# Queue orders by hand behind the head of a hybrid mLSTM and sparse-attention block

## The chip, the cores and the metric

One core of a Trainium2 chip runs the whole program. The metric is the device time of one execution in microseconds: 527.67 us for the kernel before (median of three runs, 526.49 to 528.49).

## The reference

A decoder block for 512 tokens of width 1024, all in fp32, cut to what matters:

```python
u = rmsnorm(x, norm_in)
m_q, m_k, m_v, m_o, m_z, m_if, a_q, a_k, a_v, a_z, ix_q, ix_k, ix_w = split(u @ w_in)   # 1024 x 6736
mq, mk = split(silu(causal_dwconv(concat(m_q, m_k), conv_w)))          # 4 taps
hm = mlstm_chunkwise(mq, mk, m_v, log_i, log_sigmoid(f))               # 4 heads, 128 x 256
hm = sigmoid(m_o) * rmsnorm_per_head(hm) * m_norm * silu(m_z)
score = sum_h ix_w[h] * relu(ix_q[h] . ix_k)                           # 8 indexer heads
idx = top_k(causal(score), 128)                                        # per query
ha = softmax(a_q.a_k / 8 + rel_bias, over idx) @ a_v                   # 8 heads of 64
h = x + concat(hm, ha * silu(a_z)) @ w_out                             # 1536 x 1024
h = h + (p @ w_ple) * sigmoid(h @ w_ple_gate)                          # 256 / 1024 x 1024
out = rmsnorm(h) * norm_final
```

## The kernel before

**Products.** Every operand of a product is split into a rounded high part and a low part (the difference), and a product is three matmuls of 128x128 by up to 512 columns: high by high, high by low, low by high. `dense_fm` (L200) makes four banks of one product side by side with the weights stationary, `dense_tm` (L222) does the same with the activations stationary. Weights come in slabs of 128x1024 elements through the SP queue (`load`); `split` (L143) makes a slab's high part on ScalarE (L148) and its low part on VectorE, or on GpSimd for the 14 even slabs from 8 to 34 (L149, `POOLP`). `feed` keeps loads four slabs and splits one slab ahead of the product; four slabs of a product take a bank from empty to full.

**Stages.** The head (to about 40 us) transposes x, normalises, splits u and makes the indexer's queries (`iq`) and the small product `mps` (indexer keys, gates). Then come the products mq, mk (conv inputs), mv in two halves, o and z in two halves, av, the attention's q and k by pairs of heads (`aqk`), az, the output projection `wo` in two halves, and the gate `wg` in two halves. Around them run: the indexer's scores (24 units of two matmuls, a relu, a multiply-add), its top-k (16 rounds of MAX8 and MATCH_REPLACE8 for three blocks of queries, L524 and L525), the convolutions (eight times three multiply-adds, a tanh, a multiply-add; L450 to L453), the gate sequences (scans), the mLSTM (per head four state-score steps and four numerator steps) and the attention (32 units of head and query block).

**What sets the order.** The head stands in `tc.manual_schedule`, so the compute engines run it in source order. Behind it, Tile's scheduler orders each engine's instructions by priority and by its own estimate of when they are ready; `urgent()` raises the priority of what empties a PSUM bank. In the source, side work is a list `back` of generators; each product calls `beat()` every six matmuls, which adds one credit and runs the first generator for as many steps as the credit pays (`COST_SC` 1.3 per score, `COST_CV` 1.5, `COST_TK` 1.5 per top-k pair). `weave` runs the mLSTM or the attention as the main line with two, or 1.4, six-matmul pieces of a product after each step. PSUM has four banks `mm` for the products and four banks `x` for all else. At run time each engine takes its queue strictly in the order that was fixed.

**What to follow.** `evac_iq` (L271) empties each iq bank in two halves: ScalarE copies 64 partitions (L278), VectorE subtracts (L279), then the same for the other half. L411 to L415 do so for the indexer's keys and then make the gate rows with ScalarE (`rows`, from the same bank `mps`). `evac_mv` (L537) empties a bank of mv with ScalarE (L545) and VectorE (L546). `evac_gate1` (L900) is the last stage's end: per block of 128 tokens it gates two halves of 256 columns, takes a power on GpSimd (L909), scales and stores. `values` of the attention multiplies a head's transposed weights with its values `LAG2` units after the last transpose (`flip`).

Of the kernel before, what the change touches and what calls it, by code (L numbers as in the profile page):

```python
# [47 lines left out]
def block_kernel(ctx: ExitStack, tc: tile.TileContext, x, p, w_in, b_gate, conv_w, w_out, norm_in,  # L48
# [121 lines left out]
    back, credit = [], [0.0]  # L170

    def beat():

        credit[0] += 1.0
        while back and credit[0] >= 0.0:
            cost = next(back[0], None)
            if cost is None:
                back.pop(0)
            else:
                credit[0] -= cost  # L180
        if not back:
            credit[0] = 0.0
# [17 lines left out]
    def dense_fm(nb, evac, tok0=0, name="fm"):  # L200
# [4 lines left out]
        while k0 < KT:  # L205
            h, l = piece()
            nk = h.shape[1]
            for b in range(nb):
                bs = slice(b * P, (b + 1) * P)
                for k in range(nk):  # L210
# [6 lines left out]
                    if k % 2:  # L217
                        beat()
                        yield
            k0 += nk  # L220

    def dense_tm(aH, aL, kts, evac, name="tm"):  # L222

        banks = [mm_bank(f"{name}{i}") for i in range(NT)]
        for k0 in range(0, len(kts), KP):
            sub = kts[k0:k0 + KP]
            h, l = piece()
            for i in range(NT):
# [6 lines left out]
                if k0 + KP >= len(kts):  # L235
                    evac(i, banks[i])
                beat()
                yield
# [88 lines left out]
    with tc.manual_schedule(engines={EN.PE, EN.DVE, EN.Activation, EN.Pool}):  # L327
# [33 lines left out]
        for kt in range(KT):  # L361
# [57 lines left out]
    iw_ps = x_bank("iw_ps")  # L419
    for i in range(1, NT):  # L420
        T.transpose(iw_ps[:, i * 12:(i + 1) * 12], rw[0][64:76, i * P:(i + 1) * P], ident[64:76, 64:76])
    V.tensor_copy(iwt[:, 1:, :], iw_ps[:, 12:48].rearrange("p (i c) -> p i c", c=12))

# [5 lines left out]
    tv_ps = x_bank("tv_ps")  # L429
    T.matmul(tv_ps[0:AH, :], rb, oh, start=True, stop=True)  # L430
    tv = sp.tile([P, SW], F32, tag="sH", bufs=1, name="tv")[0:AH, 0:S]
    V.tensor_copy(tv[:, 0:256], tv_ps[0:AH, 0:256])
    V.memset(tv[:, 256:S], BIG)

    tdram = dp.tile([AH, P, S], F32, name="tdram")
    nc.scalar.dma_start(tdram[:, :, 0:384], tv[:, 0:384].rearrange("h (o c) -> h o c", o=1).to_broadcast([AH, P, 384]))
# [10 lines left out]
    def conv(c, raw):  # L447
        y = mqk[c]
        for j in range(1, 4):
            V.scalar_tensor_tensor(y[:, j:], raw[:, 0:S - j], cw(3 - j, c), y[:, j:], op0=OP.mult, op1=OP.add)  # L450
        yield COST_CV
        A.activation(raw, y, AF.Tanh, scale=0.5)
        V.scalar_tensor_tensor(y, raw, 1.0, y, op0=OP.add, op1=OP.mult)  # L453
        yield COST_CV

    def evac_qk(c0):
        def go(b, ps):
# [3 lines left out]
            with urgent():  # L461
                A.activation(raw, ps, AF.Copy)
                A.activation(y, ps, AF.Copy, scale=cw(3, c))
# [12 lines left out]
    def sequences():  # L476
        A.activation(fr[1], fr[0], AF.Abs)
        A.activation(fr[2], fr[1], AF.Exp, scale=-1.0)
        A.activation(fr[1], fr[2], AF.Ln, bias=1.0)
        yield 1.0  # L480
        V.scalar_tensor_tensor(lr[2], fr[0], 0.0, fr[1], op0=OP.min, op1=OP.subtract)
        V.tensor_tensor_scan(lr[1], lr[2], lr[0], 0.0, op0=OP.add, op1=OP.max)
        yield 1.0
# [3 lines left out]
        for j in range(NT):  # L487
            n = S - j * P
            seg = ar[:, OFF[j]:OFF[j] + n]
            V.tensor_tensor_scan(seg, ones[64:76, :].to_broadcast([12, n]), lr[2][:, j * P:], 0.0, op0=OP.mult, op1=OP.add)  # L490
            V.tensor_tensor(lr[3][:, j * P:(j + 1) * P], lr[0][:, j * P:(j + 1) * P], seg[:, 0:P], OP.subtract)
            V.tensor_tensor(seg, seg, lr[1][:, j * P:], OP.subtract)
            yield 1.0
        nc.scalar.dma_start(adram, arow[72:76, 0:1280])
# [4 lines left out]
    def scores():  # L499
        for i in range(1, NT):  # L500
            n = (i + 1) * P
            sc = keep(f"sc{i}", shape=(P, n))
            for h in range(IH):
# [5 lines left out]
                A.activation(r, ps, AF.Relu)  # L509
                w = iwt[:, i, h:h + 1]  # L510
                if h == 0:
                    V.tensor_scalar(sc, r, w, None, op0=OP.mult)
                else:
                    V.scalar_tensor_tensor(sc, r, w, sc, op0=OP.mult, op1=OP.add)  # L514
                yield COST_SC
            G.affine_select(out=sc[:, i * P:], in_=sc[:, i * P:], compare_op=OP.is_ge, fill=-1e38, base=0,  # L516
                            pattern=[[-1, P]], channel_multiplier=1)
            sel[i] = sc

    def topk():  # L520
# [6 lines left out]
        for i in range(1, NT):  # L527
            V.tensor_scalar(sel[i], sel[i], -2e38, BIG, op0=OP.is_gt, op1=OP.mult)
        ended[0] = True

    back += [scores(), sequences(), topk()]
# [5 lines left out]
    def evac_mv(c):  # L537
        def go(i, ps):
# [3 lines left out]
            with urgent():  # L542
                G.memset(f(vH[i, c])[:, :, MV:], 1.0)
                G.memset(f(vL[i, c])[:, :, MV:], 0.0)
                A.activation(vH[i, c][:, :, 0:MV], src, AF.Copy)  # L545
                V.tensor_tensor(vL[i, c][:, :, 0:MV], src, f(vH[i, c])[:, :, 0:MV], OP.subtract)  # L546
# [6 lines left out]
    gc_ps = x_bank("gc_ps")  # L553
    for q, r in ((0, 3), (1, 1)):
        for i in range(NT):
            o = (q * NT + i) * 12
            T.transpose(gc_ps[:, o:o + 12], lr[r][:, i * P:(i + 1) * P], ident[64:76, 64:76])
    gc = gc_ps[:, 0:96].rearrange("p (q i c) -> p q i c", q=2, c=12)
    V.tensor_copy(gcol[:, 0], gc[:, 0, :, 8:12])

    V.tensor_scalar(gcol[:, 1], gc[:, 1, :, 8:12], -43.0, None, op0=OP.max)
    A.activation(gcol[:, 1], gcol[:, 1], AF.Exp, scale=-2.0)
    V.tensor_scalar(gcol[:, 1], gcol[:, 1], EPS, None, op0=OP.mult)
# [4 lines left out]
    def evac_o(b0):  # L568
        def ev(b, ps):
            go[b0 + b] = keep(f"go{b0 + b}")  # L570
            with urgent():
                A.activation(go[b0 + b], ps, AF.Tanh, scale=0.5)
        return ev

    def evac_z(b0):
        def ev(b, ps):
            sz = tmp("sz")
            g = go[b0 + b]
            with urgent():
                A.activation(sz, ps, AF.Tanh, scale=0.5)  # L580
                V.scalar_tensor_tensor(sz, sz, 1.0, ps, op0=OP.add, op1=OP.mult)
            V.scalar_tensor_tensor(g, g, 1.0, sz, op0=OP.add, op1=OP.mult)
# [9 lines left out]
    def split_mix(h):  # L592
        for c in (2 * h, 2 * h + 1):
            mixH[c], mixL[c] = keep(f"mixH{c}", F32R), keep(f"mixL{c}", F32R)
            A.activation(mixH[c], go[c], AF.Copy)
            V.tensor_tensor(mixL[c], go[c], f(mixH[c]), OP.subtract)
# [4 lines left out]
    def split_qk(h):  # L601
        for c in (h, 4 + h):
# [3 lines left out]
            V.tensor_tensor(qkL[c], y, f(qkH[c]), OP.subtract)  # L606

    def mlstm():
        tail = []

        def finish(h, i, hm):
            hp = x_bank("hp_ps", (P, MV))
            for q in range(2):
                T.transpose(hp[:, q * P:(q + 1) * P], hm[:, q * P:(q + 1) * P], ident)
            for q in range(2):
                g = go[2 * h + q][:, i * P:(i + 1) * P]
                V.scalar_tensor_tensor(g, hp[:, q * P:(q + 1) * P], g_m4(2 * h + q), g, op0=OP.mult, op1=OP.mult)
            if i == NT - 1:
                back.append(split_mix(h))

        for h in range(MH):
            c = h // 2
            sH = sp.tile([P, SW], F32R, tag="sH", bufs=1, name="sH")
            sL = sp.tile([P, SW], F32R, tag="sL", bufs=1, name="sL")
            for j in range(NT):
                n = S - j * P
                seg = slice(OFF[j], OFF[j] + n)
                e = tmp("e", shape=(P, n))
                nc.scalar.dma_start(e, bass.AP(tensor=adram.tensor, offset=adram.offset + h * 1280 + OFF[j],
                                               ap=[[0, P], [1, n]]))  # L630
                G.affine_select(out=e[:, 0:P], in_=e[:, 0:P], compare_op=OP.is_ge, fill=-BIG, base=0,
                                pattern=[[1, P]], channel_multiplier=-1)
                A.activation(e, e, AF.Exp, bias=gcol[:, 0, j, h:h + 1])
                ps = x_bank("st_ps", (P, n))
                js, ts = slice(j * P, (j + 1) * P), slice(j * P, S)
                first = T.matmul(ps, qkH[4 + h][:, js], qkH[h][:, ts], start=True, stop=False)
                if h == j == 0:
                    tc.keep_in_program_order(first)
                T.matmul(ps, qkH[4 + h][:, js], qkL[h][:, ts], start=False, stop=False)
                T.matmul(ps, qkL[4 + h][:, js], qkH[h][:, ts], start=False, stop=True)  # L640
                V.scalar_tensor_tensor(e, ps, 0.25 * MQK ** -0.5, e, op0=OP.mult, op1=OP.mult)
                A.activation(sH[:, seg], e, AF.Copy)
                V.tensor_tensor(sL[:, seg], e, f(sH[:, seg]), OP.subtract)
                if j == 0 and tail:
                    finish(*tail.pop(0))
                if j == NT - 1 and h < MH - 1:
                    split_qk(h + 1)
                yield
            for i in range(NT):
                ps = x_bank("nm_ps", (P, MV + 2))  # L650
                for j in range(i + 1):
                    o = OFF[j] + (i - j) * P
                    aH, aL = sH[:, o:o + P], sL[:, o:o + P]
# [326 lines left out]
```

## Time and profile before

| | before |
|---|---|
| median of three runs | 527.67 us |
| the profiled execution | 526.94 us |
| its span, first to last instruction | 524.9 us |
| TensorE busy | 498.6 us (95%), 2370 matmuls |
| VectorE busy | 349.3 us (67%) |
| ScalarE busy | 259.8 us (49%) |
| GpSimd busy | 81.3 us (15%) |
| mean granted TensorE clock | 0.989 |

TensorE is busy nearly all the time, so the time can fall only where TensorE waits, and it rises wherever a new wait is put in front of a matmul. A busy matmul in the profile overlaps the next one: a 128x512 matmul is shown with about 0.40 us, while the next starts 0.23 us behind it.

### The profile page before, as it was taken

How to read it: one execution, taken by the hardware profiler on the slowest of the kernel's cores; microseconds unless marked ns; L12 is line 12 of the kernel's file. 1: busy time of each engine (PE TensorE's matmuls, PEld its weight loads, DVE VectorE, ACT ScalarE, POOL GpSimd, SP SyncE). 2: the span in 40 equal slices, each digit the busy share in tenths (PEclk: the TensorE clock that was granted, in tenths of full speed). 3: DMA queues.
4: the chain of work that ended last, by engine and by line, in shares of the span. 5: the costliest groups of instructions: out<-in, count | busy, mean ns of one | idle time of the engine just before them, and what ended most of it. 6: DMA issues, size and time to landing. Idle time of an engine off the chain costs nothing.

```text
span 524.9 us, 6706 instructions
## 1 busy us (share of the span) xinstructions
PE 498.6 (95%) x2370; PEld 409.3 (78%) x2370; DVE 349.3 (67%) x718; ACT 259.8 (49%) x518; POOL 81.3 (15%) x110
## 2 busy tenths in 40 slices
PE   4999999894999999999999999999999999999994
PEld 3887878683878888888888787888878888888884
DVE  0945287999999827355745759979887441452744
ACT  5636183763132425465545658767875321232533
POOL 4501022231111322310101012111111000000011
PEclk9999999997999999999999999999999999999998
DMA  8352557322223224223422312121123443213012
GB/s 264 108 181 84 104 87 172 117 82 81 81 85 116 82 81 140 77 92 112 131 81 90 102 61 76 46 81 74 47 82 121 161 160 113 88 41 120 1 51 109
DMA packets 37280, 52.24 MB, mean 100 GB/s; under 512 B 4156, under 2 KB 16732, under 8 KB 37248
## 3 DMA queue, kind: packets, MB, share of 16 engines
q1 hardware_dynamic: 30464, 42.34, 25.2%
q10 hardware_dynamic: 6688, 9.46, 7.3%
q8 instruction: 18, 0.29, 0.2%
q14 instruction: 14, 0.11, 0.1%
q0 software_dynamic: 96, 0.02, 0.0%
HBM read 48.13 MB, written 3.69 MB: 99 GB/s over the span
## 4 chain that ended last, share of the span: by engine, by line
PE 74%; DVE 12%; DMA 8%; ACT 2%; issue 2%; SPq 0%; POOL 0%; POOLq 0%; ACTq 0%; DVEq 0%
DMA tdram<-tv 7%; PE wo L233 4%; PE wo L232 4%; PE wo L234 4%; PE o L212 3%; PE z L212 3%; PE z L214 3%; PE o L213 3%; PE z L213 3%; PE o L214 3%; DVE mqk L450 2%; PE aqk L212 2%; PE aqk L213 2%; PE aqk L214 2%; PE mv L232 2%
## 5 line engine op out<-in xcount | busy, mean ns | idle before, releaser
L148 ACT ACTIVATE wh<-raw 128x1024 fp32r<-128x1024 f32 x70 | 74.0, 1058 | 110.6 <-PE wo L234 36.5
L149 DVE TENSOR_TENSOR wl<-raw,wh 128x1024 fp32r<-128x1024 f32 x56 | 68.6, 1225 | 68.5 <-ACT wh L148 68.3
L149 POOL TENSOR_TENSOR wl<-raw,wh 128x1024 fp32r<-128x1024 f32 x14 | 33.8, 2415 | 134.8 <-ACT wh L148 123.4
L232 PE MATMUL wo<-wh,mixH 128*128 128x512 f32 x96 | 38.9, 405 | 0.1
L234 PE MATMUL wo<-wh,mixL 128*128 128x512 f32 x96 | 37.9, 395 | 0.0
L233 PE MATMUL wo<-wl,mixH 128*128 128x512 f32 x96 | 37.9, 395 | 0.0
L232 PE MATMUL mv<-wh,uH 128*128 128x512 f32 x64 | 26.2, 410 | 8.5 <-DVE v L546 6.6
L212 PE MATMUL aqk<-uH,wh 128*128 128x512 f32 x64 | 26.4, 413 | 0.0
L234 PE MATMUL mv<-wh,uL 128*128 128x512 f32 x64 | 26.0, 406 | 0.0
L525 DVE MATCH_REPLACE8 sc<-m,sc 128x256 f32<-128x256 f32 (+2 forms) x48 | 25.8, 544 | 0.0
L212 PE MATMUL o<-uH,wh 128*128 128x512 f32 x64 | 25.8, 402 | 0.0
L212 PE MATMUL z<-uH,wh 128*128 128x512 f32 x64 | 25.7, 402 | 0.0
L233 PE MATMUL mv<-wl,uH 128*128 128x512 f32 x64 | 25.7, 401 | 0.0
L214 PE MATMUL aqk<-uH,wl 128*128 128x512 f32 x64 | 25.4, 397 | 0.0
L214 PE MATMUL z<-uH,wl 128*128 128x512 f32 x64 | 25.4, 396 | 0.0
L213 PE MATMUL o<-uL,wh 128*128 128x512 f32 x64 | 25.4, 396 | 0.0
L214 PE MATMUL o<-uH,wl 128*128 128x512 f32 x64 | 25.3, 396 | 0.0
L213 PE MATMUL z<-uL,wh 128*128 128x512 f32 x64 | 25.3, 396 | 0.0
L213 PE MATMUL aqk<-uL,wh 128*128 128x512 f32 x64 | 25.3, 395 | 0.0
L524 DVE MAX8 m<-sc 128x8 f32<-128x256 f32 (+2 forms) x48 | 24.8, 550 | 0.2 <-POOL sc L516 0.2
L731 POOL TENSOR_SCALAR bm<-sc,tz 128x128 f32<-128x128 f32 (+1 forms) x16 | 13.7, 857 | 71.3 <-DVE ha L772 21.2
L514 DVE SCALAR_TENSOR_TENSOR sc<-relu,iwt,sc 128x256 f32<-128x256 f32 (+2 forms) x21 | 14.2, 676 | 13.7 <-ACT relu L509 12.9
(245 smaller groups left out, 1363.6 us busy)
## 6 DMA issues: line engine op xcount, KB each, us to landing
raw<-in_w_in_dram SPq DMA_DIRECT2D x44, 512.0 KB, 3.4
raw<-in_w_out_dram SPq DMA_DIRECT2D x12, 512.0 KB, 3.5
raw<-in_w_in_dram SPq DMA_DIRECT2D x16, 256.0 KB, 2.9
raw<-in_w_ple_gate_dram SPq DMA_DIRECT2D x8, 512.0 KB, 3.5
x<-in_x_dram SPq DMA_DIRECT2D x8, 256.0 KB, 5.7
xr<-in_x_dram ACTq DMA_DIRECT2D x2, 1024.0 KB, 5.6
tdram<-tv ACTq DMA_DIRECT2D x1, 1536.0 KB
tz<-tdram ACTq DMA_DIRECT2D x1, 1024.0 KB, 6.3
```

Of the source, the lines that this page charges most:

```text
L148: A.activation(h, raw, AF.Copy)
L149: (G if k in POOLP else V).tensor_tensor(l, raw, f(h), OP.subtract)
L212: T.matmul(banks[b][:, 0:nt], h[:, k, bs], uH[:, kt, tok0:], start=(kt == 0), stop=False)
L213: T.matmul(banks[b][:, 0:nt], h[:, k, bs], uL[:, kt, tok0:], start=False, stop=False)
L214: T.matmul(banks[b][:, 0:nt], l[:, k, bs], uH[:, kt, tok0:], start=False, stop=(kt == KT - 1))
L232: T.matmul(banks[i], aH(kt, i), h[:, k, :], start=first, stop=False)
L233: T.matmul(banks[i], aH(kt, i), l[:, k, :], start=False, stop=False)
L234: T.matmul(banks[i], aL(kt, i), h[:, k, :], start=False, stop=last)
L514: V.scalar_tensor_tensor(sc, r, w, sc, op0=OP.mult, op1=OP.add)
L524: V.max(out=m8, in_=sel[i])
L525: V.match_replace(out=sel[i], in_to_replace=m8, in_values=sel[i], imm_value=-3e38)
L731: G.tensor_scalar(bm[:, 0:n - 256], sel[i][:, 0:n - 256], tz[:, h, 0:1], None, op0=OP.add)
```

## The change

All four compute engines run in source order to the end of the program. The source is rewritten to be that order. `tick()` replaces `beat()` and is called every three matmuls instead of six; besides paying the generators it runs what `later(n, fn, ...)` has put off by n ticks. What empties a bank or works on a product's result is emitted that many ticks behind it. The low parts of all weight slabs go to VectorE. The first small products (`iw_ps`, `tv_ps`) become a generator `prepare`, first in `back`, that starts its transposes at the fourth tick. Top-k costs 3.0 ticks a pair, as before per time; scores cost 1.7 ticks (less than before), the convolution's steps 2.0, and the gate columns and the transposes of h become generators. The mLSTM and the attention are written as functions with fixed offsets; `LAG2` falls from 2 to 1; the attention works in one tile per unit instead of three, and makes its masks one unit ahead. The loads of the residual, of p and of the final norm move from ScalarE's queue to SP's. In the head, the slabs behind iq are fed in the turn kt == 6 instead of behind it. `evac_iq`, the key and row copies behind it, and the order of `evac_gate1` stay as written in the source.

```diff
-COST_SC, COST_CV, COST_TK, COST_MX, RATE = 1.3, 1.5, 1.5, 3.0, 1.4
+COST_SC, COST_CV, COST_TK, COST_MX, RATE_M, RATE_A = 1.7, 2.0, 3.0, 2.0, 4.0, 2.8
-POOLP = range(8, 36, 2)
-LAG1, LAG2, SW = 2, 2, 1664
+LAG1, LAG2, SW = 2, 1, 1664
...
-        (G if k in POOLP else V).tensor_tensor(l, raw, f(h), OP.subtract)
+        V.tensor_tensor(l, raw, f(h), OP.subtract)
...
+    def later(n, fn, *args):
+        heapq.heappush(due, (clock[0] + n, len(order), fn, args))
+        order.append(None)
...
+    def tick():
+        clock[0] += 1
+        while due and due[0][0] <= clock[0]:
+            _, _, fn, args = heapq.heappop(due)
+            fn(*args)
         credit[0] += 1.0
         while back and credit[0] >= 0.0:
...
-                    if k % 2:
-                        beat()
-                        yield
+                    tick()
+                    yield
...
+            if kt == 6:
+                for q in range(4):
+                    loaded.pop(q)
+                count[:] = [4, 4, 4]
+                feed(3)
         misc_step(6)
         misc_step(7)
...
+    ctx.enter_context(tc.manual_schedule(engines={EN.PE, EN.DVE, EN.Activation, EN.Pool}))
     for b in range(4):
         evac_iq(b, iqp[b])
...
+    def prepare():
+        yield 4.0
+        iw_ps = x_bank("iw_ps")
+        for i in range(1, NT):
+            T.transpose(iw_ps[:, i * 12:(i + 1) * 12], rw[0][64:76, i * P:(i + 1) * P], ident[64:76, 64:76])
+        yield 1.0
+        V.tensor_copy(iwt[:, 1:, :], iw_ps[:, 12:48].rearrange("p (i c) -> p i c", c=12))
...
         for j in range(1, 4):
             V.scalar_tensor_tensor(y[:, j:], raw[:, 0:S - j], cw(3 - j, c), y[:, j:], op0=OP.mult, op1=OP.add)
+            yield COST_CV
...
-                A.activation(r, ps, AF.Relu)
+                later(1, A.activation, r, ps, AF.Relu)
+                later(2, summed, sc, r, i, h)
...
-    back += [scores(), sequences(), topk()]
+    back += [prepare(), scores(), sequences(), topk()]
...
-                A.activation(vH[i, c][:, :, 0:MV], src, AF.Copy)
-                V.tensor_tensor(vL[i, c][:, :, 0:MV], src, f(vH[i, c])[:, :, 0:MV], OP.subtract)
+            A.activation(vH[i, c][:, :, 0:MV], src, AF.Copy)
+            later(1, V.tensor_tensor, vL[i, c][:, :, 0:MV], src, f(vH[i, c])[:, :, 0:MV], OP.subtract)
...
+        later(1, squares)
+        later(2, factor)
+        later(4, A.activation, hm, ps[:, 0:MV], AF.Copy, 0.0, st[:, 3:4])
+        later(6, turned)
...
+                        for o in (me, other):
+                            A.activation(t1[o, :], ps[me, :], AF.Copy)
+                        for o in (me, other):
+                            later(2, V.tensor_tensor, t2[o, :], ps[me, :], f(t1[me, :]), OP.subtract)
...
+            later(1, least)
+            later(2, lambda: A.activation(t, t, AF.Exp, bias=sm[:, 0:1], scale=-1.0, accum_out=sm[:, 1:2]))
+            later(3, norm)
...
-            A.activation(turned(tH, i), ps, AF.Copy)
-            V.tensor_tensor(turned(tL, i), ps, f(turned(tH, i)), OP.subtract)
+            later(1, A.activation, turned(tH, i), ps, AF.Copy)
+            later(2, V.tensor_tensor, turned(tL, i), ps, f(turned(tH, i)), OP.subtract)
...
-        for k in range(n + LAG1 + LAG2 + 1):
+        masks(*units[0])
+        for k in range(n + LAG1 + LAG2):
...
-        nc.scalar.dma_start(t, x[0, :, c * S:(c + 1) * S].rearrange("(i p) c -> p i c", p=P))
+        nc.sync.dma_start(t, x[0, :, c * S:(c + 1) * S].rearrange("(i p) c -> p i c", p=P))
...
-         attention_in(1)), lambda k: 2.0)
+         attention_in(1)), lambda k: RATE_M)
```

## Rows read from the trace of the kernel before

**Rows 1.** Waits in front of TensorE: total us, times, longest us.

```profile
PE mv L232 <- DVE v L546: 6.6, 1, 6.6
PE mv L232 <- ACT mqk L463: 1.9, 2, 1.6
PE mk L212 <- ACT mqk L463: 1.2, 1, 1.2
```

**Rows 2.** Busy time by stretch: length, PE, PEld, DVE, ACT, POOL, clock, DMA.

```profile
98.00:152.00 54.00, 46.93 (x192) 36.63 (x192) 53.87 (x111) 24.07 (x35) 13.64 (x22) 0.94 0.26 81
208.00:314.00 106.00, 105.65 (x542) 88.97 (x542) 59.76 (x117) 58.15 (x134) 15.87 (x31) 1.00 0.31 94
314.00:412.00 98.00, 96.78 (x494) 80.57 (x494) 83.01 (x217) 70.63 (x157) 13.11 (x15) 1.00 0.24 76
412.00:457.00 45.00, 45.00 (x202) 36.61 (x201) 17.45 (x20) 9.89 (x12) 0.00 (x0) 1.00 0.40 137
```

**Rows 3.** TensorE's timeline around its longest wait: start us, duration us, instruction.

```profile
128.31 0.79 PE L232 MATMUL mv<-wh,uH 128*128 128x512 f32 x1 [6.57 <-DVE v L546]
...
131.33 0.39 PE L233 MATMUL mv<-wl,uH 128*128 128x512 f32 x1
```

**Rows 4.** Costliest groups, top-k and weight low parts: busy us, mean ns.

```profile
L149 DVE TENSOR_TENSOR wl<-raw,wh 128x1024 fp32r<-128x1024 f32 x56 | 68.6, 1225 | 68.5 <-ACT wh L148 68.3
L149 POOL TENSOR_TENSOR wl<-raw,wh 128x1024 fp32r<-128x1024 f32 x14 | 33.8, 2415 | 134.8 <-ACT wh L148 123.4
...
L525 DVE MATCH_REPLACE8 sc<-m,sc 128x256 f32<-128x256 f32 (+2 forms) x48 | 25.8, 544 | 0.0
...
L524 DVE MAX8 m<-sc 128x8 f32<-128x256 f32 (+2 forms) x48 | 24.8, 550 | 0.2 <-POOL sc L516 0.2
```

**Rows 5.** Busy time by stretch of line 524 alone: length, DVE, clock, DMA.

```profile
98.00:152.00 54.00, 11.44 (x22) 0.94 0.26 81
```

**Rows 6.** VectorE and GpSimd timelines, around 79 us and 101 us.

```profile
78.95 2.89 DVE L450 SCALAR_TENSOR_TENSOR mqk<-raw,vcols,mqk 128x510 f32<-128x510 f32 x1
...
100.67 0.73 DVE L450 SCALAR_TENSOR_TENSOR mqk<-raw,vcols,mqk 128x511 f32<-128x511 f32 x1
...
78.80 2.49 POOL L149 TENSOR_TENSOR wl<-raw,wh 128x1024 fp32r<-128x1024 f32 x1 [7.44 <-ACT wh L148]
```

**Rows 7.** ScalarE, VectorE and TensorE timelines behind the head, 37 to 50 us.

```profile
37.94 0.99 ACT L278 ACTIVATE qi<-iq 64x384 fp32r<-64x384 f32 x2 [0.62 <-DVE qi L279]
...
45.28 0.59 ACT L412 ACTIVATE ik<-mps 64x512 fp32r<-64x512 f32 x1
46.63 0.59 ACT L412 ACTIVATE ik<-mps 64x512 fp32r<-64x512 f32 x1 [0.75 <-DVE ik L413]
...
48.77 0.77 ACT L414 ACTIVATE rows<-mps,gb 12x512 f32<-12x512 f32 x1
...
38.45 1.15 DVE L279 SCALAR_TENSOR_TENSOR qi<-iq,qi 64x384 fp32r<-64x384 f32 x2 [0.55 <-ACT qi L278]
...
42.65 0.40 PE L212 MATMUL mq<-uH,wh 128*128 128x512 f32 x1
```

**Rows 8.** ScalarE's timeline in the last stage.

```profile
506.23 0.66 ACT L891 ACTIVATE sgg<-wg 128x256 f32<-128x256 f32 x2 [0.99 <-PE wg L942]
...
511.83 0.66 ACT L891 ACTIVATE sgg<-wg 128x256 f32<-128x256 f32 x2 [1.01 <-PE wg L942]
...
515.93 0.36 ACT L891 ACTIVATE sgg<-wg 128x256 f32<-128x256 f32 x1
...
521.64 0.34 ACTq L919 DMA_DIRECT2D out_dram<-h  x1
```

**Rows 9.** ScalarE and VectorE timelines in the attention, one head's last transpose.

```profile
361.27 0.58 ACT L756 ACTIVATE sH<-pt_ps 128x512 fp32r<-128x512 f32 x1
...
362.58 0.68 DVE L757 TENSOR_TENSOR sL<-pt_ps,sH 128x512 fp32r<-128x512 f32 x1
```

**Rows 10.** Waits in front of ScalarE: total us, times, longest us.

```profile
ACT ak L712 <- DVE ak L713: 3.2, 3, 1.1
```

More of the change, by code (lines that the diff above doesn't have):

```diff
@@ L1 @@
+import heapq
 import math
@@ L234, in dense_tm @@
                     T.matmul(banks[i], aL(kt, i), h[:, k, :], start=False, stop=last)
[L235 to L238, printed above, removed]
+                    if last:
+                        evac(i, banks[i])
+                    tick()
+                    yield
     def run(*gens):
@@ L578, in ev @@
             g = go[b0 + b]
[L579 to L582, printed above, removed]
+            A.activation(sz, ps, AF.Tanh, scale=0.5)
+            later(1, V.scalar_tensor_tensor, sz, sz, 1.0, ps, OP.add, OP.mult)
+            later(2, V.scalar_tensor_tensor, g, g, 1.0, sz, OP.add, OP.mult)
         return ev
@@ new lines, in numerators, with squares, factor, turned @@
+    def numerators(h, i):
+        sH, sL = sHL[h]
+        c = h // 2
+        ps = x_bank("nm_ps", (P, MV + 2))
+        for j in range(i + 1):
+            o = OFF[j] + (i - j) * P
+            aH, aL = sH[:, o:o + P], sL[:, o:o + P]
+            bH, bL = vH[j, c][:, h % 2, :], vL[j, c][:, h % 2, :]
+            T.matmul(ps, aH, bH, start=(j == 0), stop=False)
+            T.matmul(ps, aH, bL, start=False, stop=False)
+            T.matmul(ps, aL, bH, start=False, stop=(j == i))
+        st = col("st", 4, bufs=4)
+        hm = tmp("hm", shape=(P, MV))
+        def squares():
+            A.activation(st[:, 0:1], ps[:, MV:MV + 1], AF.Square, scale=EPS ** 0.5)
+            A.activation(hm, ps[:, 0:MV], AF.Square, scale=MV ** -0.5, accum_out=st[:, 1:2])
+        def factor():
+            V.scalar_tensor_tensor(st[:, 2:3], st[:, 0:1], gcol[:, 1, i, h:h + 1], st[:, 1:2], op0=OP.max, op1=OP.add)
+            G.tensor_tensor(st[:, 3:4], st[:, 2:3], neghalf[:, 0:1], OP.pow)
+        def turned():
@@ L614, in finish, with gate @@
                 T.transpose(hp[:, q * P:(q + 1) * P], hm[:, q * P:(q + 1) * P], ident)
+            later(1, gate, hp)
+        def gate(hp):
             for q in range(2):
@@ L671, in mlstm @@
-        yield
-        finish(*tail.pop(0))
+                back.insert(0, split_mix(h))
+        later(1, squares)
+        later(2, factor)
+        later(4, A.activation, hm, ps[:, 0:MV], AF.Copy, 0.0, st[:, 3:4])
+        later(6, turned)
+    def mlstm():
+        steps = [(fn, h, k) for h in range(MH) for fn in (state_scores, numerators) for k in range(NT)]
+        for k, (fn, h, i) in enumerate(steps):
+            fn(h, i)
+            for ahead, prep in ((1, decays), (2, decays_load)):
+                if k + ahead < len(steps) and steps[k + ahead][0] is state_scores:
+                    later(1, prep, *steps[k + ahead][1:])
+            if fn is numerators and i == 0 and h < MH - 1:
+                later(2, split_qk, h + 1)
+            yield
@@ L805, in ev @@
             t = hs[i, c] = keep(f"h{i}_{c}")
-            with urgent():
-                V.tensor_tensor(t, ps, xr[c][:, i, :], OP.add)
+            V.tensor_tensor(t, ps, xr[c][:, i, :], OP.add)
+            if c:
+                later(2, turn_h, c, i, mm_bank("hT_ps").rearrange("p (k t) -> p k t", t=P))
         return ev
@@ L838, in block_kernel @@
+    out0 = project(0)
+    weave(attention(), chain(attention_in(2), dense_fm(4, evac_az, name="az"), attention_in(3),
+                             (next(out0) for _ in range(40))), lambda k: RATE_A)
     load_residual(0)
-    run(rest[0])
     plt = sp.tile([P, SW], F32, tag="sH", bufs=1, name="plt")
     pl = plt[:, 0:NT * DPLE].rearrange("p (i c) -> p i c", c=DPLE)
-    nc.scalar.dma_start(pl, p[0, 0].rearrange("(i p) c -> p i c", p=P))
-    pt_ps = [x_bank(f"ppt{k}") for k in range(2)]
-    for k in range(2):
-        for i in range(NT):
-            T.transpose(pt_ps[k][:, i * P:(i + 1) * P], pl[:, i, k * P:(k + 1) * P], ident)
@@ new lines, in turns @@
+    def turns():
+        for i in range(NT):
+            turn_h(0, i, x_bank("hT_ps", (P, 4, P)))
+            yield 4.0
+        for k in range(2):
+            ps = x_bank(f"ppt{k}")
+            for i in range(NT):
+                T.transpose(ps[:, i * P:(i + 1) * P], pl[:, i, k * P:(k + 1) * P], ident)
+            pH[k], pL[k] = keep(f"pH{k}", F32R), keep(f"pL{k}", F32R)
+            later(1, A.activation, pH[k], ps, AF.Copy)
+            later(2, V.tensor_tensor, pL[k], ps, f(pH[k]), OP.subtract)
+            yield 4.0
```

335 lines of the change are left out of this document (154 added, 181 removed).

## The prediction

> **What bounds the kernel now.** The page comes first: TensorE is busy 498.6 of 524.9 us, so the change can gain only where a matmul waits, and every new wait costs its full length. The view of waits in front of TensorE therefore comes second. Behind the head it has three groups that matter: the second half of mv waits 6.6 us for VectorE's copy of the first half's last bank, mv's start and its next bank wait 1.9 us for mqk on ScalarE, mk waits 1.2 us for it [rows 1]. All lie between 67 and 129 us. The stretches say why: from 98 to 152 us VectorE is busy 53.87 of 54.00 us and TensorE 46.93, while in the mLSTM (208 to 314 us) VectorE has 59.76 of 106.00 and TensorE loses 0.35 us, and in the attention (314 to 412 us) VectorE has 83.01 of 98.00 and TensorE loses 1.22 us [rows 2]. So the kernel is bound by TensorE, except for one stretch in which VectorE is full and its queue has bank copies behind convolutions, scans and top-k. The timeline of the long wait shows a second price: the matmul at 128.31 us follows 6.57 us of idle time, and the seven matmuls from there to 131.33 us take 3.02 us [rows 3]. The stretch's clock of 0.94 [rows 2] is that. At full clock a matmul follows the last by 45.00/202 = 0.223 us [rows 2], seven take 1.6; 1.4 us are lost.
>
> **The change part by part.**
>
> *The full stretch.* What VectorE does from 98 to 152 us falls. Top-k has 11.44 us of its MAX8 there [rows 5], and as much of MATCH_REPLACE8 (24.8 and 25.8 us in all [rows 4]): about 23 us go. In the new order prepare (9 ticks), scores (24 x 1.7), sequences (17), convolutions (8 x 9) and gate columns (7) stand ahead of top-k: it starts at tick 146 of the products, while mv ends at tick 128. To VectorE come five low parts (10.6 us of GpSimd's 33.8 lie here) at 1.225 us: 6.1 us [rows 4]. So 53.9 - 23 + 6 = 37 us against 46.9 us of TensorE work, about 80%. The copy of mv's bank is emitted one tick behind the bank's last matmul, and that bank is needed again about 18 matmuls later, 4 us. I take all three waits as gone: -9.7 us, and -1.4 us with the slow clock. The other end is that VectorE's backlog at the end of mv's first half still exceeds those 4 us; the nearest row is the 6.6 us wait at 100% busy, and at 80% I give back nothing.
>
> *Low parts on VectorE.* 14 x 1.225 = 17.2 us more for VectorE in all [rows 4]. Something comes back: beside GpSimd's low part at 78.80 us a convolution step on VectorE takes 2.89 us, against 0.73 us at 100.67 us [rows 6]. That is 2.2 us, nearly the 2.4 us that GpSimd's instruction lasts. It is one of seven such rows in the trace, beside seven of the 14; at 1.6 us each on average they are some 11 us, so VectorE gains about 6 us of work net (17 if none of it comes back). The cover is VectorE's idle time: in the mLSTM stretch 59.8 us, plus two low parts (2.5), plus two thirds of top-k that now lies there (34 of 48 pairs at (24.8+25.8)/48 = 1.05 us: 36 us) is 98 us of 106. That is 92%, where it was 56%.
>
> The Trainium skill bears on this ("GPSIMD Engine Reference", Specifications): GpSimd's SBUF interfaces are shared with VectorE, and it contends with VectorE instructions that have two SBUF inputs. By that rule every microsecond of GpSimd's 33.8 could stretch the convolutions, top-k replacements and subtractions beside it, and VectorE would get lighter by up to 17 us instead of heavier by 6. The trace shows it beside some of them only, so I stay with the 6, and the chance of the slow rival below hangs on this difference.
>
> *The first small products.* This is where I see a new wait. Behind the head ScalarE and VectorE empty the iq banks in turns: ScalarE's next pair starts at 37.94 us after a wait for VectorE, VectorE's pair runs from 38.45 for 1.15 us, to 39.60 [rows 7]. Code that stays as written keeps that order, so a pair takes 39.64 - 37.94 = 1.70 us. Three pairs and a single (0.5) from 37.94 end at 43.55; two rounds for the keys take 1.35 us each, the distance of 45.28 and 46.63; the gate rows take 0.77 [rows 7]. They are there at 43.55 + 2.70 + 0.77 = 47.0 us (before at 49.5, with weight high parts in between). `prepare` puts transposes that read them into TensorE's queue behind 12 matmuls of mq; in the trace the thirteenth starts at 42.65 us [rows 7]. Everything of mq is queued behind them. So TensorE stands 47.0 - 42.65 = +4.4 us. Before, the scheduler had put them behind the rows' end of 49.5 us. The clock's price after such a gap is between 0 and the 1.4 us above, which followed a longer one: +0.5.
>
> *The last stage.* ScalarE now takes a block's first tanh, its square, the second tanh, its square, the scalings and a DMA issue strictly in source order, and the next block's tanh behind them. The last block shows this chain before already: from 515.93 us to 521.64 + 0.34, 6.05 us [rows 8]. Blocks follow each other by 511.83 - 506.23 = 5.60 us. The third block's chain from 511.83 us ends at 517.9 us; the last block's first tanh waits until then, 2.0 us later than 515.93 us. If each earlier block passes on its 0.45 us as well, it is 2.9 us. I take +2.0 us.
>
> *The mLSTM and the attention.* VectorE is at 92% and about 85% there, in a fixed order. The transposes of a numerator come six ticks (4 us and the next step's matmuls) behind it, twice as long as the chain of square, factor, power and scaling needs, so I take +0.5 us, from 0 to 10. In the attention LAG2 of 1 puts a head's value products one step behind its last transposes: nine product matmuls of 0.223 us, 2.0 us. In between ScalarE copies for 0.58 us and VectorE subtracts for 0.68 us [rows 9]: 1.3 us. A 1.225 us low part [rows 4] that gets in front costs 0.5 us; over eight heads that is 0 to 4 us. Against that stand ScalarE's 3.2 us of waits for VectorE between the halves of a key tile [rows 10], which the new order (all ScalarE copies first) drops, and the 1.2 us that TensorE lost there. Net +0.5 us. The loads moved to SP's queue (residual, p, final norm) stand behind weight loads that run three slabs ahead; their users come ten or more us later, so 0, and 3 us if the residual delays the first `wo` bank.
>
> **Sum.** -9.7 - 1.4 + 4.4 + 0.5 + 2.0 + 0.5 + 0.5 = -3.2 us. The profiled execution took 526.94 us (span 524.9 and 2.0 around it), so 523.7 us. The median of the runs lies 0.7 us above it: 524.5 us.
>
> **Rivals.**
>
> 1. *No gap at the gate rows.* If the halves of a bank are not taken in turns, eight copies of 0.5 us, two of 0.6 and the rows of 0.77 let the transposes start at 42.7 us. Then 4.9 us more are gained: 519.6 us. For it: the halves are different partitions. Against it: ScalarE's waits for VectorE in rows 7. A rule of the Trainium skill ("PSUM — Partial Sum Buffer", PSUM bank collisions raise a hardware error) says that two engines may use different quadrants of one bank at once, which would allow this. The trace shows the program waiting all the same, and the change leaves that code.
> 2. *VectorE becomes the bound, slower than before.* Top-k spread over z, the mLSTM and the first `aqk` leaves VectorE 8 us of room in 106. If hand-overs and waits for tile slots eat that, each backlog goes through the banks to TensorE. Price: in the full stretch TensorE lost 7 of 54 us [rows 2]; the same share of the mLSTM's 106 us is 14 us, half of it 7. With -3.2 + 7 to 14 the time is 531 to 538 us; it decides from the point where VectorE shows 99% in that stretch. For it: 92%. Against it: the attention ran at 85% and lost 1.2 us.
> 3. *Late values.* LAG2 of 1 and bursts of `aqk` copies (2.8 us on VectorE at once) stall each head by about 0.7 us: +5 us, 529.5 us.
> 4. *The mv wait stays*, because convolutions and scans, not top-k, fill VectorE then: +7 us, 531 us. Against it: each tick now emits one convolution step at most.
>
> **How the numbers follow.** Forecast case 0.45, rival 1 0.17, rival 2 0.23, rival 3 0.10, rival 4 0.05. No change within what a measurement can tell is 0.5%, 525.0 to 530.3 us. The forecast case has a spread of 3 us and gives 0.27 faster and 0.18 same; rival 1 is faster, rival 3 mostly same, rivals 2 and 4 mostly slower. Faster 0.46, same 0.30, slower 0.24. The range reaches from rival 1 with 2 us to spare, 517 us, to rival 2's middle, 533 us; the forecast case alone is 521.5 to 527.5 us.
>
> **What would show it.** In the profile after: no wait of mv for VectorE or of mk and mv for mqk, and VectorE under 85% from mk to the end of mv; one TensorE gap of about 4.4 us near 42.7 us in front of the iw_ps transposes, released by ScalarE's rows; the last block's first tanh behind the third block's scalings, 6 us behind the third block's own first tanh instead of 4.1; VectorE 90% or more in the mLSTM, and TensorE waiting there under 2 us. The forecast is wrong if the gap is missing, or if TensorE's waits from 200 us on add up to more than 4 us.

## The result: slower by six per cent, and the profile after

The changed kernel takes 559.19 us (median of four runs, 558.78 to 559.88), the kernel before took 527.08 us beside it (four runs, 526.00 to 528.49). The ratio is 1.061 (95% interval 1.058 to 1.064). The forecast of 524.5 us was too low by 35 us, and its range ended at 533 us. The profiled execution took 559.88 us, its span is 558.1 us, its clock 0.966.

The waits in front of TensorE (total us, times, longest us), of after:

```profile
PE hp_ps L698 <- ACT hm L184: 9.8, 4, 5.5
PE iw_ps L445 <- ACT rows L427: 4.5, 1, 4.5
PE pt_ps L809 <- DVE sm L785: 3.8, 1, 3.8
...
PE lg_ps L780 <- DVE ak L184: 3.3, 1, 3.3
PE pt_ps L809 <- DVE pr L790: 3.2, 1, 3.2
...
PE pt_ps L809 <- ACT pr L184: 2.3, 3, 1.2
PE av_ps L819 <- DVE sL L184: 2.0, 1, 2.0
```

No row of mk or mv is left: the three waits of [rows 1] are gone. What has come stands in front of small transposes (`iw_ps`, `hp_ps`, `pt_ps`), logits (`lg_ps`) and values (`av_ps`). The stretches of after (columns as in [rows 2]) are mq, mv, the mLSTM beside o, z and av, the last mLSTM steps beside the first `aqk`, and the attention:

```profile
39.20:75.90 36.70, 32.23 (x130) 24.55 (x129) 15.92 (x28) 17.47 (x33) 0.29 (x1) 0.86 0.42 74
102.60:147.40 44.80, 44.80 (x194) 36.05 (x193) 35.72 (x51) 18.62 (x26) 0.20 (x2) 1.00 0.32 95
193.60:283.80 90.20, 87.26 (x440) 72.64 (x439) 77.76 (x178) 45.99 (x106) 12.81 (x24) 1.00 0.32 93
283.80:319.70 35.90, 30.42 (x145) 25.23 (x144) 26.15 (x56) 16.52 (x38) 3.23 (x7) 0.90 0.23 64
319.70:439.60 119.90, 103.50 (x497) 84.46 (x495) 82.71 (x217) 71.36 (x157) 11.85 (x16) 0.94 0.20 62
```

mv runs at TensorE's pace, with VectorE at 80%. But where TensorE waits most, in the last two rows, VectorE is at 73% and 69%: it isn't full there. The account by stage, worked out from the first and last matmul of each product in the two timelines:

| stage | before, us | after, us | difference |
|---|---|---|---|
| mq | 29.5 | 36.7 | +7.2 |
| mk and mv | 82.8 | 71.4 | -11.4 |
| o, z, av (mLSTM) | 133.1 | 136.5 | +3.4 |
| first `aqk` to the last value | 127.0 | 155.6 | +28.6 |
| from there to the last matmul | 105.5 | 108.0 | +2.5 |
| behind the last matmul | 7.4 | 10.6 | +3.2 |

With -0.4 us in the head that is 33.1 of the 33.2 us between the spans. In the fourth stage, measured against the median distance of matmuls of each shape, after has 24.1 us of gaps (before 2.6) and 7.1 us more in matmuls at the low clock (before none). The four longest gaps, 15.8 of the 24.1 us (5.5, 3.2, 3.8 and 3.3), lie at the four ends of `aqk` products, near 302, 326, 346 and 403 us; the rest are shorter ones in between, 2.0 us at most. The first of the four, in the timelines of ScalarE, VectorE, GpSimd and TensorE of after (start us, duration us, instruction, in brackets the idle time before it and what ended it):

```profile
297.82 2.40 ACT L758 ACTIVATE ak<-aqk 64x512 fp32r<-64x512 f32 x4
...
300.12 1.04 ACT L148 ACTIVATE wh<-raw 128x1024 fp32r<-128x1024 f32 x1
...
301.20 1.23 DVE L149 TENSOR_TENSOR wl<-raw,wh 128x1024 fp32r<-128x1024 f32 x1 [2.16 <-ACT wh L148]
...
301.54 0.40 PE L226 MATMUL aqk<-uH,wl 128*128 128x512 f32 x1
302.34 2.79 DVE L184 TENSOR_TENSOR ak<-aqk,ak 64x512 fp32r<-64x512 f32 x4
...
306.01 0.21 DVE L692 SCALAR_TENSOR_TENSOR st<-st,gcol 128x1 f32<-128x1 f32 x1
...
306.31 0.55 POOL L693 TENSOR_TENSOR st<-st,neghalf 128x1 f32<-128x1 f32 x1 [14.12 <-DVE st L692]
...
306.89 0.47 ACT L184 ACTIVATE hm<-nm_ps,st 128x256 f32<-128x256 f32 x1 [5.16 <-POOL st L693]
...
307.42 0.69 PE L698 MATMUL hp_ps<-ident,hm 128*128 128x128 f32 x2 [5.48 <-ACT hm L184]
```

Read it as a convoy: instructions of two engines that wait for each other, one behind the other, in queues whose order is fixed. The end of the product emits four key copies on ScalarE (2.40 us); the next slab's high part stands behind them; its low part stands on VectorE ahead of the four key subtractions (they are put off by two ticks), so VectorE idles 2.16 us with the keys ready for it; low part and subtractions take 4 us more; the mLSTM's factor comes behind all that, and behind a top-k pair, at 306.01 us, and the transposes that TensorE has next in its queue behind the factor. The same four groups of instructions follow each other at the three other ends, where VectorE idles 4.48, 3.29 and 2.64 us ahead of the low part:

```profile
323.74 1.23 DVE L149 TENSOR_TENSOR wl<-raw,wh 128x1024 fp32r<-128x1024 f32 x1 [4.48 <-ACT wh L148]
...
345.31 1.23 DVE L149 TENSOR_TENSOR wl<-raw,wh 128x1024 fp32r<-128x1024 f32 x1 [3.29 <-ACT wh L148]
...
403.87 1.22 DVE L149 TENSOR_TENSOR wl<-raw,wh 128x1024 fp32r<-128x1024 f32 x1 [2.64 <-ACT wh L148]
```

There TensorE waits for transposes of the attention (`pt_ps`) at two ends, and at the last for the subtracted keys themselves (`lg_ps`).

### The profile page after: what moved, and what is told of

Its sections match the earlier page's. It is cut to its first block, busy times and chain, and to the rows that moved or that the text cites. A ratio compares the mean times of both kernels' runs of the same rounds, so it can differ in the third digit from the quotient of the medians.

```text
span 558.1 us, 6704 instructions
## 1 busy us (share of the span) xinstructions
PE 510.5 (91%) x2370; PEld 415.5 (74%) x2370; DVE 362.9 (65%) x732; ACT 261.6 (47%) x518; POOL 45.8 (8%) x96
## 4 chain that ended last, share of the span: by engine, by line
PE 68%; DVE 15%; ACT 10%; issue 4%; DMA 2%; POOL 1%; SPq 0%; POOLq 0%; ACTq 0%; DVEq 0%
PE wo L243 4%; PE wo L245 4%; PE wo L244 4%; PE mv L245 3%; PE mv L244 3%; PE mv L243 3%; PE o L224 3%; PE z L224 2%; PE o L226 2%; PE z L225 2%; PE o L225 2%; PE z L226 2%; DVE wl L149 2%; ACT wh L148 2%; DVE ak L184 2%
## 5 line engine op out<-in xcount | busy, mean ns | idle before, releaser
L149 DVE TENSOR_TENSOR wl<-raw,wh 128x1024 fp32r<-128x1024 f32 x70 | 85.3, 1223 | 60.7 <-ACT wh L148 60.6
L148 ACT ACTIVATE wh<-raw 128x1024 fp32r<-128x1024 f32 x70 | 72.7, 1050 | 17.7 <-DMA raw<-in_w_in_dram 5.4
L243 PE MATMUL wo<-wh,mixH 128*128 128x512 f32 x96 | 40.6, 423 | 0.0
L224 PE MATMUL aqk<-uH,wh 128*128 128x512 f32 x64 | 27.8, 434 | 0.0
L793 ACT ACTIVATE pr<-pr,sm 128x128 f32<-128x128 f32 (+3 forms) x32 | 17.9, 559 | 19.5 <-DVE sm L785 19.5
L551 DVE MAX8 m<-sc 128x8 f32<-128x256 f32 (+2 forms) x48 | 26.5, 552 | 0.0
L809 PE MATMUL pt_ps<-ident,pr 128*128 128x128 f32 x80 | 15.3, 292 | 9.6 <-DVE sm L785 3.8
L245 PEld LDWEIGHTS wo<-wh,mixL 128*128 128x128 f32 x96 | 18.5, 192 | 4.5
```

The lines of the kernel that those rows point to most:

```text
L149: V.tensor_tensor(l, raw, f(h), OP.subtract)
L224: T.matmul(banks[b][:, 0:nt], h[:, k, bs], uH[:, kt, tok0:], start=(kt == 0), stop=False)
L243: T.matmul(banks[i], aH(kt, i), h[:, k, :], start=first, stop=False)
L245: T.matmul(banks[i], aL(kt, i), h[:, k, :], start=False, stop=last)
L551: V.max(out=m8, in_=sel[i])
L793: later(2, lambda: A.activation(t, t, AF.Exp, bias=sm[:, 0:1], scale=-1.0, accum_out=sm[:, 1:2]))
```

## Experiments

Every time is a median; the ratio is to the kernel before, run beside it on the same chip. "Theory A" is this convoy. "Rival 2" is the prediction's: VectorE is the bound.

**e1, low parts three ticks later** (548.11 us, ratio 1.041, 1.034 to 1.048):

```diff
-        V.tensor_tensor(l, raw, f(h), OP.subtract)
+        later(3, V.tensor_tensor, l, raw, f(h), OP.subtract) if 4 < k < 58 else V.tensor_tensor(...)
```

> The changed kernel (559.2 us) with one edit: the low part of a weight slab is emitted on VectorE three ticks behind its high part, for the slabs from mq to the first wo product. Theory A (a convoy: the four key copies on ScalarE, the slab's high part behind them, VectorE held at the low part with the key subtractions and the attention's work behind it): VectorE's waits of 2.2 to 4.5 us for wh at the four ends of aqk go, the four TensorE gaps there shrink by those 2 to 4 us each, and the time falls by 8 to 15 us, to 544 to 551 us. Theory B (VectorE is simply full since top-k is spread over the mLSTM): the order of the same work does not matter, 556 to 560 us, and the gaps stay.

**e2, key copies spread over ticks 0, 2, 4, 6, each subtraction one tick behind its copy** (545.62 us, ratio 1.036, 1.030 to 1.042):

```diff
-                    for o in (me, other):
-                        A.activation(t1[o, :], ps[me, :], AF.Copy)
-                    for o in (me, other):
-                        later(2, V.tensor_tensor, t2[o, :], ...)
+                    for q, o in enumerate((me, other)):
+                        later(4 * s + 2 * q, A.activation, t1[o, :], ps[me, :], AF.Copy)
+                        later(4 * s + 2 * q + 1, V.tensor_tensor, t2[o, :], ...)
```

> The changed kernel with one edit: the four ScalarE copies and four VectorE subtractions that empty a key bank are emitted two ticks apart, a copy and its subtraction one tick behind it, instead of four copies at once and four subtractions two ticks later. Theory A: the high part of the next slab comes behind two copies at most, each burst of 2.4 us on ScalarE and 2.8 us on VectorE is broken up, the four gaps (5.5, 3.2, 3.8, 3.3 us) fall below 1.5 us each and most of the slow clock behind them goes: 559 falls by 14 to 20 us, to 539 to 545 us. Theory B: 556 to 560 us, the gaps stay or move.

Each removes one link, and each gives back 11 to 14 of the 32 us; e2 is 0.6 us outside its expected range. The longest wait of the mLSTM's transposes, e1 and then e2:

```profile
PE hp_ps L698 <- ACT hm L184: 7.1, 4, 4.9
```
```profile
PE hp_ps L698 <- ACT hm L184: 5.0, 3, 1.9
```

So at the first end the burst is the larger link (5.5 to 1.9 us without it, to 4.9 without the low part's wait); in the attention both edits leave gaps of 2.3 us at most (e2 had been expected to leave less than 1.5 us each).

**e3, four instead of sixteen top-k rounds, so 32 keys are kept per query instead of 128** (556.39 us, ratio 1.056, 1.049 to 1.064):

> The changed kernel with 4 of the 16 rounds of top-k (the selection is then not that of the reference); VectorE has 39 us less to do, all of it before the attention. Theory B: the gaps from 200 us on go, in the mLSTM and at the first two ends of aqk above all, 535 to 542 us. Theory A: the gaps at the four ends of aqk stay within 1 us of 5.5, 3.2, 3.8 and 3.3, and only the small gaps in the mLSTM at 212 and 271 us (1.2 and 1.8 us, a top-k pair in front of the factor) go: 553 to 557 us.

```profile
PE hp_ps L698 <- ACT hm L184: 6.8, 2, 5.4
...
PE pt_ps L809 <- DVE sm L785: 3.8, 1, 3.8
PE lg_ps L780 <- DVE ak L184: 3.3, 1, 3.3
PE pt_ps L809 <- DVE pr L790: 3.2, 1, 3.2
```

With 36 of 48 top-k pairs gone the four large waits stand as before. Only two small gaps in the mLSTM (1.2 and 1.8 us, where top-k pairs stood in front of the factor) went. Rival 2 falls.

**e4, first small products** (`feed(4)` ahead of the iq copies, `yield 4.0` of `prepare` to 10.0, `COST_SC` 1.7 to 1.5; 547.24 us, ratio 1.039, 1.034 to 1.044):

> The changed kernel with the transposes of iw_ps at the tenth tick of mq instead of the fourth (scores cost 1.5 ticks instead of 1.7 in return), and the second mq slab split before the iq banks are emptied, so that it does not come behind the gate rows. Theory: the gap of 4.5 us at 42 us and the slow clock behind it (10.2 us at half clock, 4.5 us lost in matmuls) are one and the same wait, so both go: 8 to 9.5 us less, 549.5 to 551.5 us. Rival (the clock falls there for another reason, or the weights of the second slab take the place of the rows): 4 us or less.

The `iw_ps` wait is gone, and mq's stretch runs at full clock:

```profile
39.10:67.00 27.90, 27.84 (x128) 21.53 (x126) 13.75 (x25) 15.91 (x30) 0.29 (x1) 1.00 0.37 65
```

mk begins at 67.2 instead of 75.9 us: the gap of 4.5 us and the slow matmuls behind it were worth some 8 us (two score matmuls, 0.35 us, now fall behind mq). The whole edit gave 12.0 us, 2.3 more than the most that was expected. The rest shows later: o, z and av take 134.3 us instead of 136.5, and the first of the four gaps is 4.1 us instead of 5.5. That the cheaper scores, which move all side work to earlier ticks, did this isn't shown.

**e5, `LAG2` back to 2** (564.26 us, ratio 1.070, 1.067 to 1.074):

> Only LAG2 back from 1 to 2: a head's values two steps behind its last transposes. The forecast's step and its rival 3 (values come late by 0.5 to 0.7 us a head): 555 us or less. Theory A: only the gap at 382.7 us (2.0 us, values behind a low part) is of that kind, the four gaps at the aqk ends stay; 556 to 559.5 us.

Both expectations missed: it is 5 us slower. From the first `aqk` to the last value its gaps are 28.3 us, against 24.1. Of late values, which the prediction's rival 3 feared, after has one wait, `av_ps` with 2.0 us, and e5 has none; but in front of the attention's transposes e5 waits 14.4 us, after 9.3:

```profile
PE pt_ps L809 <- DVE sm L785: 6.7, 4, 3.8
...
PE pt_ps L809 <- DVE pr L790: 3.9, 2, 3.2
PE pt_ps L809 <- ACT pr L184: 3.8, 5, 1.2
```

So late values weren't the loss. Why the longer lag makes the transposes wait is left open.

**e6, the 14 low parts back on GpSimd** (`(G if k in range(8, 36, 2) else V)`; 561.48 us, ratio 1.067, 1.063 to 1.071):

> Only the low parts of the 14 even slabs 8 to 34 go back to GpSimd; all else is the changed kernel (559.2 us). Theory A (at the four aqk ends a convoy: four key copies in front of the next slab's high part on ScalarE, that slab's low part in front of the four key subtractions on VectorE): these slabs belong to mk to av, the slabs behind the four ends were VectorE's before too, so the four TensorE gaps at 300, 323, 345 and 403 us stay at 3 us and more; 557 to 561 us. Rival 2 (VectorE's 17 us more of low parts are the loss): at least 10 us come back, 549 us or less.

Nothing comes back (0.5 us above the expected range), and the waits at the four ends are the same: who makes these low parts doesn't matter. The first line of the two pages, e6 and then after, says why:

```profile
PE 512.8 (92%) x2370; PEld 418.2 (75%) x2370; DVE 365.0 (65%) x718; ACT 261.7 (47%) x518; POOL 83.7 (15%) x110
```
```profile
PE 510.5 (91%) x2370; PEld 415.5 (74%) x2370; DVE 362.9 (65%) x732; ACT 261.6 (47%) x518; POOL 45.8 (8%) x96
```

With 14 low parts fewer, VectorE is busy no less in e6. What GpSimd takes over comes back to VectorE as longer instructions beside it: convolution steps that take 0.75 us alone take 2.77 to 2.92 us there.

**e7, last stage: both tanh first, then both squares, in all blocks but the last** (557.13 us, ratio 1.058, 1.054 to 1.061):

> Only the last stage: in every block but the last both tanh come first, then the multiply-adds, then both squares. Theory (the forecast's term 'last stage': ScalarE's strict order tanh, square, tanh, square passes its lag on to the last block, measured +3.2 us from the last matmul to the end): 556 to 557.5 us, the last matmul 7.5 to 8.5 us ahead of the end. Rival (the end is set by the stores or by GpSimd's power): no change, 559 us.

As expected: the last matmul ends 8.3 us ahead of the end, instead of 10.6.

**e8, the edits of e1, e2, e4 and e7 together** (528.50 us, ten runs, ratio 1.0037, 1.0017 to 1.0057):

> Low parts three ticks later, key copies spread two ticks apart, the first small products at tick 10 with the slabs fed ahead of the iq copies, and the last stage's order, together. Theory A with the two mis-sized terms: 559.2 minus 18 to 24 (the four ends), minus 12 (first products), minus 2.5 (last stage) is 521 to 527 us, with no TensorE gap over 3 us. Rival (each edit only pushes VectorE's backlog to the next end, so the gains do not add): 532 us or more, with gaps of 3 us and more in the attention.

Four edits of source order give back 30.7 of the 32.1 us, 1.5 short of the expected range; alone they gave 11.1, 13.6, 12.0 and 2.1, together 38.8, so the gains overlap; e1 and e2 act on the same chain. From the first `aqk` to the last value 133.3 us are left of 155.6. Behind the head no gap is over 1.5 us, and no matmul ran at the low clock. The longest wait:

```profile
PE pt_ps L809 <- ACT pr L184: 3.4, 3, 1.5
```

**e11, the fixed order off behind the head, nothing else** (519.75 us, ratio 0.987, 0.984 to 0.990):

```diff
-    ctx.enter_context(tc.manual_schedule(engines={EN.PE, EN.DVE, EN.Activation, EN.Pool}))
```

> The changed kernel's text without its one line that puts all compute engines in source order behind the head: the program that orders instructions may again move what is ready in front of what is not; ticks, slabs, LAG2 and low parts stay. Theory A (the loss is the fixed order: a low part that waits for ScalarE holds up ready subtractions): the VectorE waits for wh with ready work behind them go, 525 to 540 us. Rival (the source's emission, its tick offsets and the added VectorE work cost the time, whoever orders it): 548 us or more.

This line alone is worth 39 us, and the version without it beats both kernels. It is 5 us below theory A's range: the gap at the gate rows and the lag in the last stage, which theory A left in, go too. At the same end of `aqk`, in e11:

```profile
287.91 1.06 ACT L148 ACTIVATE wh<-raw 128x1024 fp32r<-128x1024 f32 x1 [1.37 <-PE aqk L225]
...
289.00 2.41 ACT L757 ACTIVATE ak<-aqk 64x512 fp32r<-64x512 f32 x4
289.00 1.23 DVE L149 TENSOR_TENSOR wl<-raw,wh 128x1024 fp32r<-128x1024 f32 x1 [1.05 <-ACT wh L148]
...
291.44 2.79 DVE L184 TENSOR_TENSOR ak<-aqk,ak 64x512 fp32r<-64x512 f32 x4 [1.21 <-ACT ak L757]
...
294.26 0.35 DVE L691 SCALAR_TENSOR_TENSOR st<-st,gcol 128x1 f32<-128x1 f32 x2
...
295.67 0.44 PE L697 MATMUL hp_ps<-ident,hm 128*128 128x128 f32 x2 [1.11 <-ACT hm L184]
```

The burst is the same, but the high part goes ahead of it and the low part runs beside the copies. The factor follows at 294.26 us, TensorE waits 1.1 us. And its mv stretch says how little a full VectorE means by itself:

```profile
96.60:141.80 45.20, 45.09 (x192) 35.72 (x191) 45.16 (x93) 18.76 (x27) 1.88 (x19) 1.00 0.39 114
```

VectorE is busy 45.16 of 45.20 us, as in the full stretch of before [rows 2], and TensorE loses 0.1 us. At the end of mv's first half the four subtractions that free its banks start at 118.81 to 122.59 us, each behind at most one top-k pair or one convolution step; in before the last two started at 127.57 and 128.64 us, behind the scans, convolutions and top-k.

**e12 to e14, one engine alone taken out of the fixed order.** VectorE free: 544.96 us (ratio 1.035, 1.031 to 1.038).

> The changed kernel with VectorE taken out of the fixed source order behind the head (its instructions may be moved past each other again), the three other engines as they are. Theory A (a low part that waits for ScalarE stands in front of ready key subtractions): those may now go first, of the 24 us of gaps and 7 us of low clock behind 283 us most come back; the 4.5 us gap and its clock ahead of iw_ps stay, since ScalarE's rows release them: 533 to 545 us. Rival C (TensorE's own fixed order is what costs: transposes and values placed too few ticks behind what they read): 552 us or more.

TensorE free: 537.29 us (ratio 1.020, 1.016 to 1.024).

> The changed kernel with TensorE alone taken out of the fixed source order; ScalarE, VectorE and GpSimd keep it. Rival C (TensorE's own fixed order costs the time): transposes and values move behind matmuls that are ready, 518 to 528 us. Theory A: the iw_ps gap with its clock goes (9 us), but the next slab's low part is still late at the four aqk ends and its own matmuls wait for it, so part of those gaps stays: 535 to 550 us.

ScalarE free: 568.83 us (ratio 1.079, 1.076 to 1.083).

> The changed kernel with ScalarE alone taken out of the fixed source order; TensorE, VectorE and GpSimd keep it. Theory A: the next slab's high part may go ahead of the four key copies, so VectorE's low part no longer waits in front of the subtractions; about half of the 24 us of gaps and 7 us of low clock behind 283 us comes back; the gate rows may come sooner or later, so the first gap is open: 535 to 550 us. Rival C (TensorE's own order): 552 us or more.

The first two are as theory A had them, VectorE's at the upper edge; rival C, that TensorE's own order is all of it, is 9 us off in the second. From the first `aqk` to the last value about 15 and 18 us of gaps and slow matmuls are left, of 31.2 (in e13 that stretch holds 17 more matmuls of `wo`, 4.0 us, which are not counted). The third is outside theory A's range, and its time is one that rival C had (552 us or more), but rival C's cause isn't what the trace shows. Its longest wait, and ScalarE's timeline there:

```profile
PE is_ps L539 <- ACT relu L184: 17.2, 1, 17.2
```
```profile
86.44 0.41 ACTq L459 DMA_DIRECT2D tz<-tdram  x1
86.89 1.32 ACT L184 ACTIVATE relu<-is_ps 128x256 f32<-128x256 f32 x4 [12.66 <-DMA tdram<-tv]
```

One DMA issue that waits for another DMA was put ahead of four relus that TensorE, in its fixed order, needed at once. With the slow matmuls behind it mq takes 56.5 us instead of 36.7; without these 20 us e14 would take 549 us, inside theory A's range. From the first `aqk` to the last value the loss shrank from 31 to 21 us: at the first end the high part was ahead of the keys, and the four copies with the four subtractions still held up the factor (4.0 us).

## Why the prediction was wrong

**Right.** The waits of mk and mv went, and VectorE in that stretch is at the 80% that was forecast: -11.4 us for -11.1. That the lower share is what did it isn't shown: in e11 the long wait is gone too, with VectorE at 99.9%, so the place of the bank copies in the queue is enough by itself, and the sum came right partly by luck. The gap at the gate rows came where and as long as it was worked out: it is in front of `iw_ps`, 4.47 us for 4.4, with ScalarE and VectorE still taking turns at the iq banks, so rival 1 was no rival. Rival 4 didn't come.

**Mis-sized: the clock behind that gap.** It was put at +0.5 us, between 0 and 1.4. TensorE's timeline of after:

```profile
46.65 0.49 PE L445 MATMUL iw_ps<-ident,rows 12*128 12x12 f32 x3 [4.47 <-ACT rows L427]
...
55.31 0.63 PE L226 MATMUL mq<-uH,wl 128*128 128x512 f32 x1
...
56.08 0.40 PE L224 MATMUL mq<-uH,wh 128*128 128x512 f32 x1
```

From 46.65 to 55.3 us matmuls follow each other by 0.43 us, at the lower of the two levels, 1.2 GHz: +4.45 us. The upper bound had been taken from one gap [rows 3], where the low level began, by the record of the granted clock, 4.0 us ahead of the gap's end; here it began 0.9 us ahead, and it lasted 10.2 us instead of 6.8. (mq as a whole rose by 7.2 us only: 2.4 us of other waits that before has in that stretch, 1.2 of them mk's of [rows 1], are gone.)

**Mis-sized: the last stage.** +3.2 us for +2.0. The mechanism is the forecast's: the last block's first tanh follows the third block's by 6.12 us (549.02 and 542.90), as far as its own chain is long, against 4.1 in [rows 8]:

```profile
542.90 0.38 ACT L947 ACTIVATE sgg<-wg 128x256 f32<-128x256 f32 x1 [0.42 <-ACT h L983]
...
549.02 0.38 ACT L947 ACTIVATE sgg<-wg 128x256 f32<-128x256 f32 x1 [0.41 <-ACT h L983]
```

The larger value in the prediction, 2.9, in which each block passes its lag on, was the right one; e7 took 2.2 us of it out again.

**The step that failed: "the mLSTM and the attention", +1.0 us, measured +32.** For the mLSTM it set the six ticks (4 us and more) against the factor's own chain alone; for the attention it set one low part (1.225 us) against the slack of nine matmuls; and it set VectorE's busy share against the room. The share was no surprise: VectorE was even below its 92% and 85%. The forecast's own sign of being wrong came up, waits from 200 us on of more than 4 us: they are 25 us. But in a fixed order the length of a chain decides, not the share. The copies (2.4 us), the high part (1.05), the low part (1.23) and the subtractions (2.8) are 7.5 us in a row, at each of four ends, and TensorE had work for 2.7 to 6 us of its own from the first copy on before it needed the chain's end. The trace of before had all four durations in its groups by line (588 ns a copy, 1058 the high part, 687 a subtraction, and in [rows 4] 1225 the low part):

```profile
L148 ACT ACTIVATE wh<-raw 128x1024 fp32r<-128x1024 f32 x70 | 74.0, 1058 | 110.6 <-PE wo L234 36.5 <-PE o L213 17.1 <-PE wg L234 11.5
...
L712 ACT ACTIVATE ak<-aqk 64x512 fp32r<-64x512 f32 x16 | 9.4, 588 | 3.4 <-DVE ak L713 3.2
...
L713 DVE TENSOR_TENSOR ak<-aqk,ak 64x512 fp32r<-64x512 f32 x16 | 11.0, 687 | 2.0 <-ACT ak L712 1.6
```

Rival 3 named the burst, and priced it at 0.7 us a head, 5 us in all; it named it without the high and low part that queue with it, and without what the clock adds: 7.1 us in this stage.

**Rival 2** gave the right sign for the wrong reason. It was to decide where VectorE shows 99%; at the losses it shows 69% to 86%, three quarters of top-k less leave them standing (e3), and e11 shows 99.9% without a loss. The low parts didn't make VectorE 6 us heavier either: with them it is busy 2.1 us less than without (e6).

**What the change is worth without its order.** e11 keeps the tick loop, the low parts and `LAG2`, and is 7 us faster than before: mk and mv take 72.5 us (before 82.8), the other stages are each within 1.5 us of before. That is the forecast's first term alone. In it, neither the rows' gap nor the tail nor the convoy comes up. What stays open: e5's 5 us, the 3 to 4 us that e4 gave back behind mq, and how the four ends' loss divides exactly between the low part's wait and the burst, since e1 and e2 overlap. The +2.5 us between the last value and the last matmul had no term in the sum: 0.7 us are three matmuls of `wo` that come later, the rest are short waits of 0.4 us at most.

## What to carry to other kernels

Before all engines are put in source order, write down for each bank end what is emitted on each queue at that point, add the durations along the queues, and place what TensorE does next behind that sum: a busy share of 70% says nothing about a chain of 7.5 us. An instruction that waits for another engine (a low part for its high part, a DMA issue for a DMA) is put behind what is ready, not in front of it. And price a TensorE gap at up to about twice its length (4.47 and 4.45 us here), since the matmuls behind it may run at half clock.

## What was not expected of the hardware

Short gaps cost clock too, and unevenly: behind the 4.47 us gap in mq the slow matmuls cost 4.45 us, behind the 6.57 us gap of before 1.4 us [rows 3], and the same gap in e12 (4.48 us) 3.1 us. In e8, where no gap behind the head is over 1.5 us, no matmul there was at the low level; in e13 no gap there is longer either, and yet the granted clock fell to the low level at 49.2, 363.2 and 390.5 us; the first time, behind a gap of 1.15 us, the slow matmuls cost 1.4 us.
